# A transformer block on one core: the router's logits taken from scaled rows while the output projection still runs

## Chip, cores and metric

One core of a Trainium2 chip runs the whole block in one launch. The metric is the device time of that launch in microseconds (us), lower is better. The engines are TensorE (PE, its weight loads PEld), VectorE (DVE), ScalarE (ACT), GpSimd (POOL) and SyncE (SP), which issues nearly all transfers.

## What is computed

256 tokens of width 2048 go through an adaptive layer norm, a token mixer (window attention and a gated delta rule, merged and put through `w_out`), a residual norm, a second adaptive norm, a mixture of 32 experts with two experts for each token, and a last residual norm.

```python
u = layer_norm(x) * (1.0 + sc1) + sh1
mix = token_mixer(u, ...)                        # ends in merged @ w_out
x = layer_norm(DEEPNORM_ALPHA * x + g1 * mix, ln1_g, ln1_b)      # "first residual norm"
u = layer_norm(x) * (1.0 + sc2) + sh2
ffn = hier_moe(u, ...)       # router logits -> group, two experts -> gate_up, silu, down
x = layer_norm(DEEPNORM_ALPHA * x + g2 * ffn, ln2_g, ln2_b)
```

Everything is float32. The expert weights are 384 tiles of 1 MB; every expert is computed with 64 slots.

## The kernel before

Tokens lie in two tiles of 128 partitions (`NT` = 2). The stages around the change:

- **Output projection** (`out_todo`, L929). Four column blocks c of 512; each is made of 16 half tiles of `w_out`, and each half tile is split by ACT (`wh`, L288) and DVE (`wl`, L289) into a high and a low part, so that PE computes three products for each (`mx`, L293 to L295). `run` (L375) walks the 32 jobs; while it runs, five expert tiles are fetched ahead (`load_ahead`) and the last part of the modulation (`ada`, L236) is summed on DVE.
- **evac(c)** (L1007). Out of PSUM: `mt` = product times g1 (L1011), `x` = ALPHA x + mt (L1012), sums for the norm (`bn_stats`, L1013). At c = 1 `router_prep` (L983) turns the modulation and the router weights into `br`, `ncs`, `wsel`.
- **The chain to the router** (L1038 to L1092). Once all four blocks are there: mean and 1/std of each token (`both`), then for each c and token tile `x` = (x - mean) ln1_g (L1059) and `x` = x rs + ln1_b (L1060), transposes (L1063), copies into `uq` (L1064), squares on ACT (L1066), logit products (L1053), and a second mean and 1/std from the products' extra column and from the squares. The logits `L` come out at L1090.
- **Routing** (L1128 to L1161): tied maxima, masks, ranks; then `slots` (L1208) makes the 0/1 matrices `G`.
- **xh** (L1101): the twice normalised rows, on ACT, and `g2b` (L1005).
- **Experts.** 16 pairs. `gather` (L1229) makes `XT` = xh-transposed by G in four steps of 8 products (L1236); `gate_up` (L1247) uses 16 weight tiles, `down` (L1288) eight. For pair 0 the gather's steps 1 to 3 stand before k = 2, 6 and 10 of `gate_up` (`GS`). For the other pairs the gather runs between `gate_up` and `down` of the pair before.

Expert tiles go through 17 buffers in a fixed rotation: four of `wp` (L74), six of `wm` (L1325), seven of `wm1` (L1338), issued in program order of use. Five of `wm1` hold the tiles fetched ahead; two hold `l1`, the rows ln1_g and ln1_b (loaded at L1019), until L1060 has read them.

The framework (Tile) orders the instructions of each engine at build time: of those whose inputs are ready it takes the one that stands first in the program. The kernel writes orders by hand only through `run`.

Of the kernel before, what the change touches and what calls it, by code (L numbers as in the profile page):

```python
# [16 lines left out]
P = 128  # L17
# [46 lines left out]
def tile_block(ctx: ExitStack, tc: tile.TileContext, A: dict, out: bass.AP, dbg=None, upto=99):  # L64
# [17 lines left out]
    rows = cp.tile([16, 512], F32, name="rows")  # L82
# [8 lines left out]
    nc.scalar.dma_start(rows, A["lnr"])  # L91
# [70 lines left out]
    def pg(nm):  # L162
        return ps_g.tile([P, 512], F32, tag="g", name=nm)
# [749 lines left out]

    mo = ctx.enter_context(tc.tile_pool(name="mo", bufs=1, reuse_waits="tile"))
# [5 lines left out]
    rw = rwx.enter_context(tc.tile_pool(name="rw", bufs=1, side=R, reuse_waits="tile"))  # L920
    ahead = []

    def load_ahead():
        n = len(ahead)
        w = wm1.tile([P, 2048], F32, tag="w1", name="w1")
        nc.sync.dma_start(w, A["w_gu"][n])
        ahead.append(w)
# [32 lines left out]
    sb = mo.tile([P, NT, 4, 6], F32, name="sb")  # L960
    g2b = mo.tile([P, D], F32, name="g2b")
    L = mo.tile([P, NT, 36], F32, name="L")
    br = rw.tile([P, 36], F32, name="br")
    ncs = rw.tile([P, 36], F32, name="ncs")
    wsel = rw.tile([P, 37], F32, name="wsel")
    rin = rw.tile([P, RW], F32, name="rin")
    nc.sync.dma_start(rin, A["router"])

    def RI(n):
# [4 lines left out]
    l1 = []  # L974
# [7 lines left out]
    def router_prep():  # L982
        mod2 = rw.tile([P, KT, 2], F32, name="mod2")  # L983
# [5 lines left out]
        V.tensor_tensor(wr, wr, sc2c.unsqueeze(2).to_broadcast([P, KT, 64]), op=MUL)  # L989
        G.memset(wr[:, :, 36:37], 1.0)  # L990
        V.tensor_add(wsel, ident[:, 0:37], ident[:, 64:101])
        rc = rw.tile([36, 2], F32, name="rcol")
        V.tensor_copy(rc, pb[:36, 0:2])
        pb = ps_w.tile([P, 512], F32, tag="ws", name="pbr2")
        for j in range(2):
            T.matmul(pb[:, 64 * j:64 * j + 36], rc[:, j:j + 1].to_broadcast([36, P]), ident[:36, :36],
                     start=True, stop=True)
        V.tensor_tensor(br, pb[:, :36], RI("br"), op=ADD)
        V.tensor_scalar(ncs, pb[:, 64:100], -1.0, None, op0=MUL)

    def g2_rows(cs):
        for c in cs:
            p = ps_w.tile([P, 512], F32, tag="ws", name=f"g2{c}")
            spread(p, mrs[5], 32 * c)
            SC.copy(g2b[:, c * 512:(c + 1) * 512], p)  # L1005

    def evac(c, ps):  # L1007
        cs = slice(c * 512, (c + 1) * 512)
        for t in range(NT):
            mt = rw.tile([P, 512], F32, tag="mt", name=f"mt{c}{t}", bufs=2)  # L1010
            V.tensor_tensor(mt, ps[t], gc[c], op=MUL)  # L1011
            V.scalar_tensor_tensor(x[t][:, cs], x[t][:, cs], ALPHA, mt, op0=MUL, op1=ADD)  # L1012
            V.bn_stats(sb[:, t, c, :], x[t][:, cs])  # L1013
        if c < 3:
            g1_row(c + 1)
        if c == 0:
            for q in (0, 4):
                w = wm1.tile([P, D], F32, tag="w1", name=f"l1{q}")
                nc.sync.dma_start(w, A["lnr"][q:q + 4, :].rearrange("a b -> (a b)").partition_broadcast(P))  # L1019
                l1.append(w)  # L1020
        if c == 1:
            while 4 not in mrs:
                next(ada)
            router_prep()

    g1_row(0)
    out_todo()
    run(None, 0, ADA[4])
# [9 lines left out]

    for _ in ada:
        pass  # L1040
    mv, rs = both(sb, "b")
    s2 = mo.tile([P, NT, 4], F32, name="s2")
    nb1 = mo.tile([P, 1], F32, name="nb1")
    V.tensor_reduce(nb1, l1[1], axis=AX.X, op=ADD)
    V.tensor_scalar(nb1, nb1, -1.0 / D, None, op0=MUL)
    pl = ps_w.tile([P, 512], F32, tag="ws", name="pl")
    uqs = []

    def logits(c):
        for k in range(4):  # L1050
            K = 4 * c + k
            j = 64 * (k % 2)
            T.matmul(pl[j:j + 64, :S], wr[:, K, :], uqs[c][:, k, :], start=(K < 2), stop=(K >= KT - 2))  # L1053

    for c in range(4):
        cs = slice(c * 512, (c + 1) * 512)
        uq = rw.tile([P, 4, S], F32, tag="uq", name=f"uq{c}", bufs=2)
        for t in range(NT):
            V.scalar_tensor_tensor(x[t][:, cs], x[t][:, cs], mv[:, t, 0:1], l1[0][:, cs], op0=SUB, op1=MUL)  # L1059
            V.scalar_tensor_tensor(x[t][:, cs], x[t][:, cs], rs[:, t], l1[1][:, cs], op0=MUL, op1=ADD)  # L1060
            p = pg(f"ut{t}{c}")
            for k in range(4):
                T.transpose(p[:, k * P:(k + 1) * P], x[t][:, (4 * c + k) * P:(4 * c + k + 1) * P], ident)  # L1063
            SC.copy(uq[:, :, t * P:(t + 1) * P], p.rearrange("p (k s) -> p k s", k=4))  # L1064
            scr = rw.tile([P, 512], F32, tag="mt", name=f"sq{c}{t}", bufs=2)
            SC.activation(scr, x[t][:, cs], AF.Square, bias=nb1, accum_out=s2[:, t, c:c + 1])  # L1066
        uqs.append(uq)
        if c:
            logits(c - 1)
    logits(3)  # L1070
# [3 lines left out]
    for t in range(NT):  # L1074
        T.matmul(pl[:, 64 * t:64 * t + 37], lt[:, t * P:(t + 1) * P], wsel, start=True, stop=True)
    for t in range(NT):
        dump(f"x1{t}", x[t])

    mv, dv, sv, rs = [mo.tile([P, NT, 1], F32, name=f"{n}c") for n in ("mv", "dv", "sv", "rs")]
    V.tensor_reduce(sv[:, :, 0], s2, axis=AX.X, op=ADD)  # L1080
    py = pl[:, 0:128].rearrange("p (t c) -> p t c", t=NT)[:, :, 36:37]
    V.tensor_scalar(dv, py, 1.0 / D, nb1, op0=MUL, op1=ADD)
    V.tensor_scalar(mv, py, 1.0 / D, None, op0=MUL)
    V.tensor_tensor(dv, dv, dv, op=MUL)
    V.scalar_tensor_tensor(sv, sv, 1.0 / D, dv, op0=MUL, op1=SUB)
    SC.activation(rs, sv, AF.Sqrt, bias=epsl)
    V.reciprocal(rs, rs)
    for t in range(NT):
        V.scalar_tensor_tensor(L[:, t, :], ncs, mv[:, t, 0:1], pl[:, 64 * t:64 * t + 36], op0=MUL, op1=ADD)
        V.scalar_tensor_tensor(L[:, t, :], L[:, t, :], rs[:, t], br, op0=MUL, op1=ADD)  # L1090
    nmr = mo.tile([P, NT, 1], F32, name="nmr")
    V.scalar_tensor_tensor(nmr, mv[:, :, 0:1], -1.0, rs, op0=MUL, op1=MUL)  # L1092
    rs2 = rs
# [6 lines left out]
    for t in range(NT):  # L1100
        SC.activation(xh[t], x[t], AF.Identity, bias=nmr[:, t], scale=rs2[:, t])  # L1101
        g2_rows((2 * t, 2 * t + 1))
# [53 lines left out]
    for t in range(NT):  # L1156
        p = pm(f"rk{t}")
        T.matmul(p[:, :NE], C("lt"), msk[:, t, :], start=True, stop=(t == 0))
        if t:
            T.matmul(p[:, :NE], ones, msk[:, 0, :], start=False, stop=True)  # L1160
        V.scalar_tensor_tensor(pos[:, t, :], msk[:, t, :], -4096.0, p[:, :NE], op0=MUL, op1=ADD)  # L1161

# [66 lines left out]
    def gather(pr, Gs):  # L1229
        XT = mo.tile([P, KT, P], F32, tag="XT", name=f"XT{pr}")  # L1230

        def step(kq):
            p = pm(f"xg{pr}_{kq}")
            for k in range(4):
                for t in range(NT):
                    T.matmul(p[:, k * P:(k + 1) * P], xh[t][:, (4 * kq + k) * P:(4 * kq + k + 1) * P],  # L1236
                             Gs[t].bitcast(F32), start=(t == 0), stop=(t == NT - 1))
            for k in range(4):
                K = 4 * kq + k
                if kq % 2:  # L1240
# [280 lines left out]
def pack(inp):  # L1521
# [44 lines left out]
    wr = np.concatenate([wr, np.zeros((D, 28), np.float32)], 1)  # L1566
# [33 lines left out]
```

## Time and profile before

| | |
|---|---|
| median of 3 runs | 1809.97 us (1809.28 to 1811.17) |
| profiled execution | 1810.3 us, span 1808.4 us, clock 0.985 |
| PE, PEld busy | 1726.9 us (95%), 1106.4 us (61%) |
| DVE, ACT busy | 895.6 us (50%), 516.9 us (29%) |
| HBM read | 624.65 MB, 347 GB/s over the span |

Busy time is that of one profiled execution. A busy PE is not PE at its peak, since the ends of its pipelined products are modelled; the starts tell its pace.

### The profile page before, as it was taken

The page shows a single profiled execution, that of the slowest core. Times are in us where ns is not written, and L with a number is a line of the kernel's source. Part 1 is how long each engine was busy: PE and PEld are TensorE (multiplying, and loading weights), DVE is VectorE, ACT ScalarE, POOL GpSimd, SP SyncE. Part 2 cuts the span into 40 slices and gives each one's busy share as a digit, 9 for nine tenths or more (in the row PEclk, how much of TensorE's full clock was granted, in tenths as well). Part 3 has the DMA queues.
Part 4 walks back from the last instruction along what each step waited for, and adds up shares of the span by engine and source line. Part 5 has one row for each costly group of instructions (what it writes and reads, how often), then busy time and mean ns, then how long its engine had stood idle before and what let it go on. Part 6 is the DMA issues. An engine that isn't in the chain of part 4 may idle for free. (4 is left out here: it accounts for less than half of the span.)

```text
span 1808.4 us, 27501 instructions
## 1 busy us (share of the span) xinstructions
PE 1726.9 (95%) x11526; PEld 1106.4 (61%) x11526; DVE 895.6 (50%) x1454; ACT 516.9 (29%) x955; POOL 43.4 (2%) x50
## 2 busy tenths in 40 slices
PE   7999998999999999997999999999999999999995
PEld 4779887898999999885434444344434444343331
DVE  3356897798788788666223322233213321233026
ACT  3334798336333544435100110011100110011101
POOL 0000001103000000000000000000000000000000
PEclk8999998999999999999999999999999999999998
DMA  9995565465788688978999999999999999999995
GB/s 397 420 362 209 199 254 192 163 258 205 282 288 319 233 303 317 364 263 323 368 421 420 421 420 420 421 421 420 420 421 420 421 420 421 420 420 421 394 422 223
DMA packets 87287, 628.58 MB, mean 348 GB/s; under 512 B 9828, under 2 KB 9828, under 8 KB 11252
## 3 DMA queue, kind: packets, MB, share of 16 engines
q1 hardware_dynamic: 86832, 626.43, 86.4%
q8 instruction: 92, 1.51, 0.3%
q10 hardware_dynamic: 328, 0.36, 0.1%
q14 instruction: 35, 0.29, 0.0%
HBM read 624.65 MB, written 2.10 MB: 347 GB/s over the span
## 5 line engine op out<-in xcount | busy, mean ns | idle before, releaser
L1257 PE MATMUL pg<-w,XT 128*64 128x512 f32 x1024 | 278.5, 599 | 3.4 <-DMA w<-in_w_gu 2.5
L1257 PE MATMUL pu<-w,XT 128*64 128x512 f32 x1024 | 275.5, 594 | 0.0
L293 PE MATMUL ws<-uh,wh 128*128 128x256 f32 x896 | 259.4, 290 | 2.3 <-ACT wh L288 2.3
L288 ACT CAST wh<-w 128x1024 fp32r<-128x1024 f32 x176 | 184.6, 1050 | 257.3 <-PE ws L294 122.2
L295 PE MATMUL ws<-uh,wl 128*128 128x256 f32 x896 | 254.0, 284 | 4.3 <-DVE wl L289 4.3
L294 PE MATMUL ws<-ul,wh 128*128 128x256 f32 x896 | 253.7, 283 | 0.0
L289 DVE TENSOR_TENSOR wl<-w,wh 128x1024 fp32r<-128x1024 f32 x176 | 218.7, 1243 | 52.4 <-PE mx L294 22.8
L1295 PE MATMUL pd<-w,hT 128*64 128x512 f32 x1016 | 234.1, 599 | 0.8 <-DVE hT L1272 0.8
L1264 DVE TENSOR_TENSOR hs<-hs,pu 128x512 f32<-128x512 f32 x16 | 11.0, 687 | 430.3 <-PE pu L1257 430.3
L293 PEld LDWEIGHTS ws<-uh,wh 128*128 128x128 f32 x896 | 169.3, 189 | 12.4 <-issue 7.8
L295 PEld LDWEIGHTS ws<-uh,wl 128*128 128x128 f32 x896 | 169.1, 189 | 6.6 <-DVE wl L289 5.7
L236 DVE SCALAR_TENSOR_TENSOR acc<-w,csil,acc 128x1024 f32<-128x1024 f32 x128 | 165.3, 1307 | 12.6 <-DMA w<-in_w_ada 12.3
L294 PEld LDWEIGHTS ws<-ul,wh 128*128 128x128 f32 x896 | 169.3, 189 | 1.4 <-issue 1.2
L1257 PEld LDWEIGHTS pu<-w,XT 128*64 128x64 f32 x1024 | 77.8, 137 | 146.6 <-issue 146.6
L1257 PEld LDWEIGHTS pg<-w,XT 128*64 128x64 f32 x1024 | 72.5, 137 | 133.6 <-issue 114.0
L1236 PEld LDWEIGHTS xg<-G,xh 128*128 128x128 f32 x1024 | 120.0, 193 | 41.3 <-issue 25.8
L1295 PEld LDWEIGHTS pd<-w,hT 128*64 128x64 f32 x1016 | 66.4, 136 | 124.1 <-issue 109.2
L1236 PE MATMUL xg<-G,xh 128*128 128x128 f32 x1024 | 131.7, 283 | 6.9 <-DVE x L1312 3.5
L1263 ACT ACTIVATE hs<-pg 128x512 f32<-128x512 f32 x16 | 9.6, 598 | 438.5 <-PE pg L1257 438.5
L410 ACT CAST dh<-pd 128x512 fp32r<-128x512 f32 x64 | 37.6, 587 | 281.3 <-DVE pd L1298 160.8
L1298 DVE SCALAR_TENSOR_TENSOR pd<-pd,wsl,g2b 128x512 f32<-128x512 f32 x64 | 48.5, 758 | 104.0 <-PE pd L1295 104.0
L1312 DVE TENSOR_TENSOR x<-x,cb 128x512 f32<-128x512 f32 x120 | 76.9, 682 | 22.7 <-PE cb L1308 22.7
(391 smaller groups left out, 2363.8 us busy)
## 6 DMA issues: line engine op xcount, KB each, us to landing
w<-in_w_gu SPq DMA_DIRECT2D x256, 1024.0 KB, 19.8
w<-in_w_dn SPq DMA_DIRECT2D x127, 1024.0 KB, 19.8
w<-in_w_ada SPq DMA_DIRECT2D x64, 1024.0 KB, 5.1
w<-in_w_in SPq DMA_DIRECT2D x56, 1024.0 KB, 5.1
wx<-in_w_a SPq DMA_DIRECT2D x18, 1024.0 KB, 11.1
w<-in_w_pab SPq DMA_DIRECT2D x16, 1024.0 KB, 6.0
w<-in_w_out SPq DMA_DIRECT2D x16, 1024.0 KB, 4.9
w<-in_w_a SPq DMA_DIRECT2D x14, 1024.0 KB, 10.7
```

Source lines behind the costliest of these rows:

```text
L236: V.scalar_tensor_tensor(acc[:, hc], w[:, hc], csil[:, k:k + 1], acc[:, hc], op0=MUL, op1=ADD)
L288: SC.copy(h, w)
L289: V.tensor_tensor(lo, w, h.bitcast(F32), op=SUB)
L293: T.matmul(p, a[0], b[0], start=first, stop=False)
L294: T.matmul(p, a[0], b[1], start=False, stop=False)
L295: T.matmul(p, a[1], b[0], start=False, stop=last)
L410: SC.copy(h, src)
L1236: T.matmul(p[:, k * P:(k + 1) * P], xh[t][:, (4 * kq + k) * P:(4 * kq + k + 1) * P], Gs[t].bitcast(F32), start=(t == 0), stop=(t == NT - 1))
L1257: T.matmul(dst[64 * e:64 * e + 64, :], XT[:, k, 64 * e:64 * e + 64], we[:, e * 1024 + hv * 512:e * 1024 + hv * 512 + 512], start=(k == 0), ...
L1295: T.matmul(pd[64 * e:64 * e + 64, :], hT[:, f, 64 * e:64 * e + 64], we[:, (2 * (f % 2) + e) * 512:(2 * (f % 2) + e + 1) * 512], start=(f = ...
L1298: V.scalar_tensor_tensor(pd, pd, ws, g2b[:, cs], op0=MUL, op1=MUL)
L1312: V.tensor_tensor(x[t][:, cs], x[t][:, cs], p, op=ADD)
```

## The change

The rows that go to the router are no longer normalised first. `evac(c)` now writes `x` = (x - mu0) ln1_g, with mu0 the mean of the first column block alone, and takes the squares of that; transposes and logit products of block c are put into the jobs of block c + 1 (`beside`). What the true mean, 1/std and ln1_b add to the logits is put in afterwards with constants that `router_prep` computes (`cons`, from extra columns of the router weights), in 15 small DVE instructions ahead of the second root. `router_prep` moves from c = 1 to c = 0. The first gather takes the unfinished `x` with G times a token factor, and adds what is missing with a product of 17 rows (`rows`, `r17`); behind each of its four steps `x` is finished on DVE and `xh` written on ACT. `l1` is therefore read until pair 0's third step. The PSUM pools are opened anew ahead of the projection (four `pg` buffers instead of five, one for `pl`).

```diff
+    early = [wm1.tile([P, 2048], F32, tag="w1", name="w1") for _ in AHEAD]
...
+    for q in (0, 4):
+        w = wm1.tile([P, D], F32, tag="w1", name=f"l1{q}")
+        nc.sync.dma_start(w, A["lnr"][q:q + 4, :].rearrange("a b -> (a b)").partition_broadcast(P))
+        l1.append(w)
...
     def router_prep():
+        V.tensor_reduce(nb1, l1[1], axis=AX.X, op=ADD)
...
+        for k in range(KT):
+            T.matmul(pb[:39, 0:3], wr[:, k, :39], wr[:, k, 36:39], start=(k == 0), stop=(k == KT - 1))
...
+        for j in range(4):
+            T.matmul(pb[:, 64 * j:64 * j + 39], rc[:, j:j + 1].to_broadcast([39, P]), ident[:39, :39],
                      start=True, stop=True)
...
     def evac(c, ps):
...
             V.bn_stats(sb[:, t, c, :], x[t][:, cs])
+            if c == 0:
+                V.bn_aggr(mu0[:, t, :], sb[:, t, 0:1])
+            V.scalar_tensor_tensor(x[t][:, cs], x[t][:, cs], mu0[:, t, 0:1], l1[0][:, cs], op0=SUB, op1=MUL)
+            SC.activation(mt, x[t][:, cs], AF.Square, accum_out=s2[:, t, c:c + 1])
+            todo.append(lambda t=t: turn_part(c, t))
...
+        if c == 2:
+            SC.activation(epst, epsl, AF.Sqrt)
+        todo.append(lambda: logits(c))
...
-    run(None, 0, ADA[4])
+    run(beside(), 1.0, ADA[4], drain=False)
...
-            V.scalar_tensor_tensor(x[t][:, cs], x[t][:, cs], mv[:, t, 0:1], l1[0][:, cs], op0=SUB, op1=MUL)
-            V.scalar_tensor_tensor(x[t][:, cs], x[t][:, cs], rs[:, t], l1[1][:, cs], op0=MUL, op1=ADD)
...
+    g2_rows(range(4))
...
+    stt(one(q2), col(37), nd, one(sv))
+    stt(one(pa), lambda t: cons[:, 1], nd, lambda t: pt[t])
+    stt(one(pa), one(pa), rs, lambda t: cons[:, 2])
+    stt(one(q2), one(q2), rs, col(38))
+    V.tensor_scalar(nm, pa[:, :, 36:37], -1.0 / D, None, op0=MUL)
+    stt(one(q2), pcol(37), nd, one(q2))
+    V.tensor_tensor(dv, nm, nm, op=MUL)
+    stt(one(q2), one(q2), rs, pcol(38))
+    V.scalar_tensor_tensor(sv, q2, 1.0 / D, dv, op0=MUL, op1=SUB)
+    SC.activation(rs2, sv, AF.Sqrt, bias=epsl)
...
-        SC.activation(xh[t], x[t], AF.Identity, bias=nmr[:, t], scale=rs2[:, t])
...
+    def first_gather(Gs):
...
+            V.tensor_scalar(Gp[:, t], Gs[t].bitcast(F32), ag[:, t], None, op0=MUL)
...
+                T.matmul(p[:17, kq * P:(kq + 1) * P], vk[:, t, 17 * kq:17 * kq + 17], Gs[t].bitcast(F32),
+                         start=(t == 0), stop=(t == NT - 1))
...
+        SC.copy(r17, p[:17, :])
...
+            for t in range(NT):
+                T.matmul(p, x[t][:, (4 * kq + k) * P:(4 * kq + k + 1) * P], Gp[:, t], start=(t == 0), stop=False)
+            T.matmul(p, rows[:, k * P:(k + 1) * P], r17[:, kq * P:(kq + 1) * P], start=False, stop=True)
...
+                V.scalar_tensor_tensor(x[t][:, cs], l1[0][:, cs], nd[:, t], x[t][:, cs], op0=MUL, op1=ADD)
+                V.scalar_tensor_tensor(x[t][:, cs], x[t][:, cs], rsb[:, t], l1[1][:, cs], op0=MUL, op1=ADD)
+                SC.activation(xh[t][:, cs], x[t][:, cs], AF.Identity, bias=nmr[:, t], scale=rs2[:, t])
```

## Rows read from the trace of the kernel before

**Rows 1.** Busy time by stretch: us, busy of each engine, PEclk, DMA share, GB/s

```profile
800.00:810.00 10.00, 10.00 (x44) 7.92 (x43) 7.62 (x10) 4.05 (x5) 0.00 (x0) 1.00 0.72 254
...
850.00:855.00 5.00, 4.50 (x22) 3.05 (x23) 1.55 (x10) 2.50 (x8) 0.00 (x0) 0.68 0.01 2
...
898.00:900.00 2.00, 2.00 (x14) 1.21 (x15) 1.52 (x5) 0.21 (x1) 0.00 (x0) 1.00 0.06 25
902.00:904.00 2.00, 2.00 (x12) 0.63 (x10) 0.90 (x2) 0.59 (x1) 0.00 (x0) 1.00 0.83 344
...
1200.00:1400.00 200.00, 195.41 (x962) 82.14 (x960) 52.01 (x101) 18.49 (x40) 0.00 (x0) 1.00 1.01 420
```

**Rows 2.** ACT in order of time: start, duration, once a pair after gate_up

```profile
1003.84 0.60 ACT L1263 ACTIVATE hs<-pg 128x512 f32<-128x512 f32 x1 [30.12 <-PE pg L1257]
...
1524.78 0.60 ACT L1263 ACTIVATE hs<-pg 128x512 f32<-128x512 f32 x1 [29.89 <-PE pg L1257]
1584.70 0.60 ACT L1263 ACTIVATE hs<-pg 128x512 f32<-128x512 f32 x1 [31.93 <-PE pg L1257]
```

**Rows 3.** Waits of PEld from 1500 to 1600: us, times, longest

```profile
PEld pg L1257 <- DMA w<-in_w_gu: 4.4, 4, 1.4
```

**Rows 4.** PE in the projection, in order of time

```profile
777.52 0.39 PE L295 MATMUL mx<-wh,ml 128*128 128x512 f32 x1
777.84 0.63 PE L996 MATMUL pbr<-cst,rcol 36*128 36x36 f32 x4
778.40 0.50 PE L293 MATMUL mx<-wh,mh 128*128 128x512 f32 x1
...
757.82 1.28 PE L988 MATMUL pbr<-mod,rin 128*36 128x2 f32 x32
759.03 0.50 PE L294 MATMUL mx<-wl,mh 128*128 128x512 f32 x1
```

**Rows 5.** The projection's first product, one near the end, the last, of 384

```profile
730.61 0.79 PE L293 MATMUL mx<-wh,mh 128*128 128x512 f32 x1
...
820.05 0.39 PE L295 MATMUL mx<-wh,ml 128*128 128x512 f32 x1
...
822.77 0.39 PE L295 MATMUL mx<-wh,ml 128*128 128x512 f32 x1
```

**Rows 6.** The chain from the projection to the first gate_up, in order of time

```profile
822.52 1.37 DVE L1011 TENSOR_TENSOR mt<-mx,gc 128x512 f32<-128x512 f32 x2 [1.28 <-PE mx L295]
...
835.82 1.42 DVE L1060 SCALAR_TENSOR_TENSOR x<-x,rsb,l 128x512 f32<-128x512 f32 x2
...
837.15 1.09 PE L1063 MATMUL ut<-cst,x 128*128 128x128 f32 x8
...
838.17 1.94 PE L1053 MATMUL pl<-uq,rin 128*64 128x256 f32 x14
...
841.25 0.22 DVE L1082 TENSOR_SCALAR dvc<-plt,nb 128x2 f32<-128x2 f32 x1 [1.43 <-PE plt L1075]
...
842.46 0.42 DVE L1090 SCALAR_TENSOR_TENSOR L<-L,rsc,br 128x36 f32<-128x36 f32 x2
...
842.87 0.22 DVE L1128 TENSOR_REDUCE mg<-L 128x1 f32<-128x4 f32 x2
...
847.81 0.49 DVE L1208 TENSOR_TENSOR G<-pos,cst 128x128 fp32r<-128x128 f32 x2
848.82 3.44 PEld L1236 LDWEIGHTS xg<-G,xh 128*128 128x128 f32 x20 [0.31 <-ACT xh L1101]
...
853.05 1.15 PE L1257 MATMUL pg<-w,XT 128*64 128x512 f32 x4 [0.50 <-ACT XT L1244]
```

**Rows 7.** Pair 0 on PE: step 3 of the gather

```profile
874.04 2.05 PE L1236 MATMUL xg<-G,xh 128*128 128x128 f32 x16
```

**Rows 8.** SP's issues: start, time until the last of the group, tile

```profile
717.73 14.57 SPq L74 DMA_DIRECT2D w<-in_w_out  x5
732.35 0.90 SPq L917 DMA_DIRECT2D x<-in_x  x2
```

More of the change, by code (lines that the diff above doesn't have):

```diff
@@ L81, in tile_block @@
     cst = cp.tile([P, CW], F32, name="cst")
-    rows = cp.tile([16, 512], F32, name="rows")
+    rows = cp.tile([17, 512], F32, name="rows")
+    nc.gpsimd.memset(rows, 1.0)
     pre = ExitStack()
@@ L924, in load_ahead @@
         n = len(ahead)
-        w = wm1.tile([P, 2048], F32, tag="w1", name="w1")
-        nc.sync.dma_start(w, A["w_gu"][n])
-        ahead.append(w)
+        nc.sync.dma_start(early[n], A["w_gu"][n])
+        ahead.append(early[n])
     def out_todo():
@@ L1001, in g2_rows, with turn_part @@
+        V.tensor_tensor(br, cons[:, 3, :36], RI("br"), op=ADD)
     def g2_rows(cs):
         for c in cs:
-            p = ps_w.tile([P, 512], F32, tag="ws", name=f"g2{c}")
+            p = pg(f"g2{c}")
             spread(p, mrs[5], 32 * c)
             SC.copy(g2b[:, c * 512:(c + 1) * 512], p)
+    uqs, todo = [], []
+    pl = ps_l.tile([P, 512], F32, name="pl")
+    def turn_part(c, t):
+        if t == 0:
+            uqs.append(rw.tile([P, 4, S], F32, tag="uq", name=f"uq{c}", bufs=2))
+        p = ps_w.tile([P, 512], F32, tag="ws", name=f"ut{t}{c}")
+        for k in range(4):
+            T.transpose(p[:, k * P:(k + 1) * P], x[t][:, (4 * c + k) * P:(4 * c + k + 1) * P], ident)
+        SC.copy(uqs[c][:, :, t * P:(t + 1) * P], p.rearrange("p (k s) -> p k s", k=4))
@@ L1007, in evac, with logits @@
+    def logits(c):
+        for k in range(4):
+            K = 4 * c + k
+            j = 64 * (k % 2)
+            T.matmul(pl[j:j + 64, :S], wr[:, K, :], uqs[c][:, k, :], start=(K < 2), stop=(K >= KT - 2))
     def evac(c, ps):
@@ L1024, in evac, with beside @@
             router_prep()
+        if c == 2:
+            SC.activation(epst, epsl, AF.Sqrt)
+        todo.append(lambda: logits(c))
+    epst = mo.tile([P, 1], F32, name="epst")
+    def beside():
+        while True:
+            if todo:
+                todo.pop(0)()
+            yield
     g1_row(0)
     out_todo()
-    run(None, 0, ADA[4])
+    run(beside(), 1.0, ADA[4], drain=False)
     def both(sv, nm):
@@ L1037, in both @@
         return mv, rs
+    for f in todo:
+        f()
+    mv, rs = both(sb, "b")
     for _ in ada:
         pass
[L1041 to L1058, printed above, removed]
-            V.scalar_tensor_tensor(x[t][:, cs], x[t][:, cs], mv[:, t, 0:1], l1[0][:, cs], op0=SUB, op1=MUL)
-            V.scalar_tensor_tensor(x[t][:, cs], x[t][:, cs], rs[:, t], l1[1][:, cs], op0=MUL, op1=ADD)
[L1061 to L1070, printed above, removed]
     lt = rw.tile([P, S], F32, name="lt")
@@ L1084, in tile_block @@
[L1084 to L1092, printed above, removed]
@@ L1093, in tile_block @@
-    rs2 = rs
+        T.matmul(pl[:, 64 * t:64 * t + 39], lt[:, t * P:(t + 1) * P], wsel, start=True, stop=True)
+    g2_rows(range(4))
+    nd, sv, q2, nm, dv, rs2, nmr, ag = [mo.tile([P, NT, 1], F32, name=f"{n}c")
+                                       for n in ("nd", "sv", "q2", "nm", "dv", "rs2", "nmr", "ag")]
+    pa = rw.tile([P, NT, 39], F32, name="pa")
+    pt = [pl[:, 64 * t:64 * t + 39] for t in range(NT)]
+    V.tensor_reduce(sv[:, :, 0], s2, axis=AX.X, op=ADD)
+    V.tensor_tensor(nd, mu0[:, :, 0:1], mv[:, :, 0:1], op=SUB)
@@ L1099, in tile_block @@
     xh = [mo.tile([P, D], F32, name=f"xh{t}") for t in range(NT)]
-    for t in range(NT):
-        SC.activation(xh[t], x[t], AF.Identity, bias=nmr[:, t], scale=rs2[:, t])
-        g2_rows((2 * t, 2 * t + 1))
+    vk = mo.tile([P, FF], F32, tag="hs", name="vk")[:, :NT * 68].rearrange("p (t c) -> p t c", t=NT)
+    G.memset(vk, 0.0)
     pps.close()
@@ L1440, in tile_block @@
             Gs = slots(pr, pair(pr)[0])
-            XT, step = gather(pr, Gs)
+            XT, step = first_gather(Gs)
             step(0)
```

99 lines of the change are left out of this document (67 added, 32 removed).

## The prediction, made before the changed kernel ran

> **What bounds the kernel now.** I read the busy time by stretch first. From 904 us to 1782 us the transfers never rest: 420 GB/s, DMA share 1.01, with PE busy for 195 of 200 us beside them [rows 1]. So both are near their limit, and the next view has to tell which one sets the pace. The reader is to look at the instruction that ends `gate_up`, once a pair: nine periods from 1003.84 to 1524.78 take 57.88 us each, the next takes 59.92 [rows 2]. A pair needs 24 tiles of 1024 KB; at 420 GB/s that is 24 x 2.50 = 59.9 us. So PE runs faster than the supply for eleven pairs, eats the stock of up to 17 loaded tiles, and is held by the transfers from pair 12 on, where PEld waits 4.4 us for `w_gu` [rows 3]. The end therefore hangs on the time at which the transfers became continuous. That is 902.3: in the 2 us before 900 they stood (share 0.06), and in 902 to 904 they had 0.83 of the time [rows 1]. They stood because all 17 buffers were full while PE did pair 1's gather, and went on when PE had used pair 0's first `down` tile. **So the place that decides is the time at which PE reaches pair 0's `down`;** what shifts that shifts the whole rest. The other rest of the transfers, 850 to 855 (0.01), is also that of full buffers, and loading earlier is not to be had there.
>
> Three stretches of PE lead there. In the output projection PE is full (10.00 of 10) [rows 1]: its products start 0.2267 us apart (12 of them from 820.05 to 822.77), 384 of them are 87.1 us, and the stretch from 730.61 to 823.0 is 92.4 us [rows 5]; the router's and `gc`'s pieces fill nearly all the rest. In the chain, from 823.0 to 853.05, PE mostly waits for DVE [rows 6]. In pair 0 PE is full again.
>
> **The change, part by part.** I call 823.0 E.
>
> *Moved into the projection* (PE, full, so on the path). 24 of the 32 transposes: eight take 1.09 us with the last one's own 0.34 in it, so 0.108 each [rows 6], 2.6 us. 24 of the 32 logit records: fourteen in 1.94 with a last one of 0.39, so 0.12 each [rows 6], 2.9 us. The second set of router products, 32 records of few columns like those at 757.82, which cost 1.21 [rows 4]: 1.2 us. Four more records of `pbr3`: 0.5 us. Breaking into the stream costs too: between 777.52 and 778.40 four records took 0.88 - 0.23 = 0.65 [rows 4], about 0.13 more than their pace, and there are nine such groups, 1.2 us. Sum **8.4 us**. Bounds: 7.2 without the breaks; above, DVE gets 1.4 us more work in each `evac` and `router_prep` comes in c = 0, so that PE may wait for `wl` up to 1 us in each of three blocks, 11.4. I take 8.4, since PE's own rows carry it.
>
> The Trainium skill (TensorE: Matmul & The Clock Gate, Part 4: PE-mode transpose) gives about 275 ns for a transpose in a kernel. By that, an estimate, 24 of them would be 6.6 us and the stretch 4 us longer than by the row. The row decides: the durations overlap, and the pace is 0.108.
>
> *The chain on DVE.* Before: from the first `mt` (822.52) to the last L1060 (837.24), 14.7 us, and 4.0 more until the transposes, copies, logits and selection let L1082 start at 841.25 [rows 6]. After: two each of `mt`, `x`, `bn_stats` and the scaled step, at 0.64 us, 5.1 us, so E + 4.6; the tail of 4.0 stays as it is for the last block: E + 8.6 instead of E + 18.25. *Gain 9.65.* Then the corrections: L1082 to the first maximum took 1.62 us [rows 6]. Now nine dependent steps stand before the root, mostly of two small instructions; two of 36 columns take 0.42, a single narrow one 0.13 to 0.22 [rows 6], so about 2.2 us, and root, reciprocal and the last two 1.15: 3.35. *Loss 1.7.* Six more small ones for `vk` and `ag` ahead of `G`, partly in PE's turns there, *loss 0.3*, and the root may queue behind a `g2b` copy on ACT, *loss 0.2*. `G` stands at E + 17.8 instead of E + 25.3 (848.30): **gain 7.5**. Bounds 6.5 to 8.5.
>
> *From G to the first gate_up.* Before 4.75 us (848.30 to 853.05), with 20 loads in 3.44, 0.17 each at a clock that fell to 0.68 in that stretch [rows 1, 6]. After: 16 records for the 17 rows, a copy on ACT that the first row product waits for (0.2 beyond the products before it), 24 records instead of 16, and `XT`'s first part, 0.5. The wait for `xh` on ACT goes. 40 records at 0.12 are 4.8, at 0.17 6.8 us; PE is idle longer before it than now, so I take the second: 7.5 in all, **loss 2.75**, bounds 0.9 and 4.5. First `gate_up`: E + 25.3 against E + 30.05, 4.75 earlier.
>
> *Pair 0.* Each of steps 1 to 3 gets eight more records. Sixteen take 2.05 us with a last one of 0.28, 0.118 each [rows 7], so 0.95 for eight: **2.85 us** for three steps, on a full PE. The DVE and ACT work behind each step (four DVE instructions of 0.7, two on ACT) lies beside `gate_up`, where DVE and ACT have over 80% free; if that cover were gone, `XT` of the next step would come up to 2.8 us late.
>
> *Transfers.* `l1` now keeps two of the 17 buffers until step 3 is done. 15 tiles instead of 17 are there when PE starts. That costs nothing as long as SP passes the two loads that need those buffers and goes on with `wp` and `wm`, which come free from k = 5 on: at 2.50 us a tile they keep the transfers busy, and by pair 0's `down` the buffers are full again, about 2.5 us ahead. That SP's order does so is seen at the projection: the two loads of x, first in the program, wait for room, and five `w_out` loads stand before them [rows 8]. The memset ahead of `rows`, the new PSUM pools and the early Sqrt table go with nothing on the path; their bound is 0.3 us.
>
> Sum at pair 0's `down`: +8.4 - 4.75 + 2.85 = **+6.5 us**, and as much at the end. 1810.3 (span 1808.4 and 1.9 around it) + 6.5 = 1816.8; the profiled run is 0.3 above the median, so 1816.5. With the bounds of each (7.2 to 11.4; gain 3 to 7.6; 2.5 to 3), its own range is 1812.5 to 1821.
>
> **The rivals.** A measurement of this kernel can tell 0.2%, 3.6 us, from no change.
>
> *A: SP stands at `l1`'s buffers.* If the loads keep their program order, the sixth load after the fetched stock (tile 20) waits for step 3 and its DVE work: PE's step 3 began 21 us after the first `gate_up` [rows 6, 7] and would end at 26, DVE 3.5 later, landing begins 1.5 after that, at 31. First `gate_up` is then at 856.7, so tile 20 starts at 887.7; continuous from 902.3 with tile 33 means 869.8 for tile 20 now. 17.9 us later, and nothing gives it back: 1828. For it: the rotation is fixed and SP is one queue. Against: [rows 8].
>
> *B: the moved pieces cost little, and the kernel is not slower.* Place: the projection, at each `evac`. If the pieces fill time in which PE would wait for DVE's `wl` anyway, as 2.2 us of `gc` and router products did around 757.82 [rows 4], half of the 8.4 is covered: 4.2 - 4.75 + 2.85 = +2.3, 1812. It decides as soon as the projection grows by less than 5.5 us; free altogether it gives 1808, with a full clock at the first gather 1806. Against: outside that place the products stand 0.2267 apart without a hole. A rule speaks for it: the Trainium skill (Trainium Kernel Development and Optimization, Performance Expectations) calls matmul busy time a bad metric and asks for the share of the weight loads; that is 79% in this stretch, so a fifth would be free for the 8.4 us, and the result would be B's. The spacing of the starts in the rows speaks against it.
>
> *C: the pieces are not where the program puts them,* but run after E, where PE has 4.6 us of waiting for DVE. Then the projection grows by the router's 1.9 alone and the chain by what does not fit into the wait, 1 to 2 us: 1.9 + 1.5 - 4.75 + 2.85 = +1.5, 1811.5. Against: they become ready a block earlier, and what is ready and first in the program goes first.
>
> **How the numbers follow.** Forecast 0.70 (1816.5), A 0.12 (1828), B 0.13 (1812, with 0.05 of it at 1806 or below), C 0.05 (1811.5). The range 1810 to 1825 holds nearly all of the forecast, C and most of B, and leaves out A and B's lowest part. Slower by over 0.2%: the forecast without its lowest tenth, and A, 0.75; faster by over 0.2%: B's lowest part, 0.06; within: 0.19.
>
> **What would show it.** Right: the projection, first to last product, 8 us longer, with transposes and `pl` records between its products; first maximum 12 us after its end, `G` at 18, `gate_up` at 25; pair periods unchanged; the transfers' second rest still there, about 6 us later. Wrong: a projection under 98 us (B, C), or SP standing at a `wm1` load while `wp` is free and a rest of over 8 us during pair 0's `gate_up` (A). If DVE is what the first gather waits for, the corrections were priced too low.

## The result, and the profile after

The changed kernel takes 1828.76 us (median of four runs, 1823.19 to 1834.54) against 1809.62 for the kernel before beside it: ratio 1.0105, interval 1.0073 to 1.0138. It is slower, as forecast, but by 19 us where 6.5 were forecast, outside the range of 1810 to 1825. The profiled execution is the slowest of the four: 1834.5 us, span 1832.7, mean granted clock 0.979. One execution of one variant below was disturbed (4794 us) and is left out.

All stations below are counted from the projection's first product, since its start differs from profile to profile: 728.8 and 731.1 in two of the changed kernel as it is, 728.8 to 736.4 over its variants, 730.6 to 733.0 in the three of the kernel before and its variants. What moves it is open.

| us after the projection's first product | before | after | difference | forecast |
|---|---|---|---|---|
| last product of the projection | 92.2 | 105.5 | +13.3 | +8.4 |
| first maximum of the router | 112.3 | 118.3 | +6.1 | |
| `G` | 117.2 | 124.0 | +6.8 | +0.9 |
| first `gate_up` | 122.4 | 137.3 | +14.9 | +3.65 |
| pair 0's `down` | 168.1 | 192.1 | +24.0 | +6.5 |
| end of the span | 1077.8 | 1101.7 | +23.9 | +6.5 |

The loss is complete at pair 0's `down`, and from there to the end nothing is added. ACT once a pair, after `gate_up` (start, duration), against [rows 2]:

```profile
1028.24 0.60 ACT L1345 ACTIVATE hs<-pg 128x512 f32<-128x512 f32 x1 [30.13 <-PE pg L1339]
...
1491.03 0.60 ACT L1345 ACTIVATE hs<-pg 128x512 f32<-128x512 f32 x1 [29.89 <-PE pg L1339]
1549.60 0.60 ACT L1345 ACTIVATE hs<-pg 128x512 f32<-128x512 f32 x1 [30.60 <-PE pg L1339]
```

1028.24 against 1003.84 is 24.4 later, 1549.60 against 1524.78 is 24.8. The eight periods up to 1491.03 are 57.85 us each, as before; then the supply of weights sets the pace, as before (the next but one takes 60.84, against 59.92).

**The projection.** The four blocks (from `mt` to `mt`) took 23.83, 22.59 and 22.66 us before; now 32.17, 24.87 and 24.87. So block 1 alone lost 8.3 us, the other two 2.3 and 2.2. Block 1 in order of time on DVE (first the kernel before, then the changed one), on PE, and by stretch (us, busy of PE, PEld, DVE, ACT, POOL, PEclk, DMA share, GB/s):

```profile
751.25 2.28 DVE L1044 TENSOR_REDUCE nb<-l 128x1 f32<-128x2048 f32 x1
...
757.03 2.35 DVE L289 TENSOR_TENSOR wl<-w,wh 128x1024 fp32r<-128x1024 f32 x2
```

```profile
752.17 2.28 DVE L1000 TENSOR_REDUCE nb<-l 128x1 f32<-128x2048 f32 x1
...
760.37 1.21 DVE L290 TENSOR_TENSOR wl<-w,wh 128x1024 fp32r<-128x1024 f32 x1
```

```profile
760.61 1.33 PE L1017 MATMUL pbr<-rin 128*39 128x3 f32 x32 [1.26 <-ACT mt L1061]
761.87 0.79 PE L295 MATMUL mx<-wl,mh 128*128 128x512 f32 x1
...
766.21 0.63 PE L296 MATMUL mx<-wh,ml 128*128 128x512 f32 x1
766.64 0.63 PE L294 MATMUL mx<-wh,mh 128*128 128x512 f32 x1
```

```profile
755.00:760.00 5.00, 4.34 (x41) 3.40 (x39) 5.00 (x13) 2.38 (x4) 0.00 (x0) 1.00 1.01 421
760.00:765.00 5.00, 4.39 (x44) 3.89 (x45) 3.30 (x7) 1.21 (x4) 0.00 (x0) 0.69 0.59 202
765.00:770.00 5.00, 5.00 (x19) 4.10 (x18) 0.64 (x2) 1.54 (x3) 0.00 (x0) 0.63 0.15 61
```

From 752.17 to 760.37 DVE writes no `wl`: the sum over `l1`, `evac(0)` with its new scaled step, and the router's instructions stand in one row of 8.2 us. Before, the sum over `l1` stood at the same place, and the row was 5.8 us long; the 2.4 us are the scaled step with its mean and the router's DVE work, which came behind two `wl` then (it stood at c = 1 in the program, but ran in this block all the same). PE runs out of work around 760 (1.26 idle), and the granted clock falls to 0.69 and 0.63 in the next two stretches; the products at 766 start 0.43 apart instead of 0.2267 [rows 5].

**The chain.** DVE and PE from the logits' selection to the first `gate_up`, and the busy time by stretch there:

```profile
846.19 0.34 DVE L1115 SCALAR_TENSOR_TENSOR q2c<-plt,ndc,svc 128x1 f32<-128x1 f32 x2 [1.89 <-PE plt L1103]
...
849.38 0.21 DVE L1168 TENSOR_REDUCE mg<-L 128x1 f32<-128x4 f32 x2
```

```profile
853.45 1.06 PE L1198 MATMUL rk<-msk,cst 128*128 128x32 f32 x4 [7.29 <-DVE msk L1178]
...
855.51 3.57 PE L1297 MATMUL rk<-G,vk 128*17 128x128 f32 x16 [0.57 <-DVE G L1255]
859.01 1.22 PE L1304 MATMUL xg<-Gp,x 128*128 128x128 f32 x4
860.16 0.79 PE L1305 MATMUL xg<-r,rows 17*128 17x128 f32 x2
860.89 1.22 PE L1304 MATMUL xg<-Gp,x 128*128 128x128 f32 x4
...
868.38 1.98 PE L1339 MATMUL pg<-w,XT 128*64 128x512 f32 x4
```

```profile
850.00:855.00 5.00, 1.49 (x6) 1.35 (x6) 4.03 (x40) 1.58 (x3) 0.00 (x0) 0.50 1.00 415
...
860.00:865.00 5.00, 5.00 (x17) 3.71 (x16) 0.00 (x0) 0.00 (x0) 0.00 (x0) 0.50 0.00 0
865.00:870.00 5.00, 5.00 (x16) 3.01 (x17) 2.74 (x4) 2.90 (x6) 0.00 (x0) 0.50 0.02 3
```

The reader is to see two things. PE stood for 7.29 us ahead of the ranks, and the granted clock falls to 0.50, that is 1.2 GHz, during this wait (0.72 in 845 to 850) and stays there until 871.1, after the first `gate_up` products: every record of the first gather runs at 1.2 GHz. And PE takes the gather as four records of 128 rows and two of 17 rows in turn, 1.88 us for each such six.

**Pair 0's step 1,** at full clock, beside which [rows 7] had sixteen records in 2.05 us:

```profile
873.28 0.71 PE L1304 MATMUL xg<-Gp,x 128*128 128x128 f32 x4
873.93 0.48 PE L1305 MATMUL xg<-r,rows 17*128 17x128 f32 x2
874.34 0.71 PE L1304 MATMUL xg<-Gp,x 128*128 128x128 f32 x4
```

1.055 us for each six, four times a step: 4.2 us where 1.98 + 0.95 was forecast. The starts within a six tell where it goes: records of one shape follow each other every 0.112 us, six of them 0.67; the other 0.385 falls on the two changes of shape, 0.19 each.

### The profile page after: what moved, and what is told of

It reads as the page before. It is cut to its first block, busy times and chain, and to the rows that moved or that the text cites. A ratio compares the mean times of both kernels' runs of the same rounds, so it can differ in the third digit from the quotient of the medians.

```text
span 1832.7 us, 27708 instructions
## 1 busy us (share of the span) xinstructions
PE 1747.9 (95%) x11610; PEld 1121.1 (61%) x11610; DVE 902.6 (49%) x1485; ACT 517.9 (28%) x963; POOL 46.1 (3%) x53
## 5 line engine op out<-in xcount | busy, mean ns | idle before, releaser
L1377 PEld LDWEIGHTS pd<-w,hT 128*64 128x64 f32 x1016 | 66.4, 136 | 124.0 <-issue 109.4
L1283 PEld LDWEIGHTS xg<-G,xh 128*128 128x128 f32 x960 | 112.8, 194 | 37.8 <-issue 22.7
L1283 PE MATMUL xg<-G,xh 128*128 128x128 f32 x960 | 123.3, 283 | 6.1 <-DVE x L1394 3.5
```

Of the source, the lines that this page charges most:

```text
L1377: T.matmul(pd[64 * e:64 * e + 64, :], hT[:, f, 64 * e:64 * e + 64], we[:, (2 * (f % 2) + e) * 512:(2 * (f % 2) + e + 1) * 512], start=(f = ...
```

## The experiments

One table holds the stations of every kernel that ran (us after the first product of the projection; the last column is from `down` to the end of the span).

| kernel | last product | first maximum | G | first gate_up | down | down to end | median us | ratio to before |
|---|---|---|---|---|---|---|---|---|
| before | 92.2 | 112.3 | 117.2 | 122.4 | 168.1 | 909.6 | | |
| after | 105.5 | 118.3 | 124.0 | 137.3 | 192.1 | 909.6 | 1828.8 | 1.0105 |
| l1 held in the kernel before | 92.2 | 112.6 | 117.6 | 122.8 | 168.4 | 910.0 | 1813.2 | 1.0011 |
| rows last | 105.4 | 118.3 | 124.0 | 132.5 | 181.4 | 909.5 | 1824.8 | 1.0080 |
| pieces late | 97.5 | 113.9 | 119.6 | 129.4 | 182.7 | 909.9 | 1826.6 | 1.0096 |
| router early | 103.1 | 115.9 | 121.6 | 131.4 | 184.7 | 910.3 | 1829.4 | 1.0102 |
| PE kept busy | 104.1 | 117.2 | 122.3 | 130.0 | 183.2 | 909.6 | 1826.1 | 1.0096 |
| no 17-row products | 105.7 | 118.5 | 124.2 | 130.0 | 175.7 | 912.5 | 1824.1 | 1.0068 |
| three mended | 103.1 | 116.2 | 121.3 | 129.0 | 179.2 | 910.2 | 1821.6 | 1.0061 |
| all late | 95.8 | 111.2 | 116.3 | 122.5 | 172.9 | 909.6 | 1815.7 | 1.0025 |
| changed again | 104.1 | 116.9 | 122.6 | 135.9 | 190.9 | 909.6 | 1829.6 | 1.0112 |
| x finished early | 95.9 | 115.1 | 120.1 | 124.8 | 171.7 | 908.5 | 1812.4 | 1.0020 |
| before, PE kept busy | 92.2 | 112.5 | 121.1 | 128.4 | 175.3 | 908.4 | 1815.9 | 1.0031 |
| x behind G | 95.0 | 111.1 | 116.3 | 120.3 | 166.4 | 908.9 | 1810.4 | 0.9992 |

The last column stays between 908.4 and 910.3 while `down` moves by 26 us, but for one kernel (912.5, explained there). That the time of pair 0's `down` sets the end, the base of the forecast, is shown.

**Rival A: `l1`'s buffers held, in the kernel before.** The fetched tiles get their buffers early, and two small additions behind step 3 read `l1`, so that two buffers are kept until then and nothing else changes.

```diff
+                    if pr == 0 and K == 15:
+                        for j in range(2):
+                            V.tensor_tensor(junk, l1[j][:, 0:1], p[:, 511:512], op=ADD)
```

> The kernel before, with one thing of the change: the five buffers for the tiles fetched ahead are taken first and l1's two last, and both rows of l1 are read once more, a single column each, by DVE behind step 3 of pair 0's gather, so that their buffers come free only then. Rival A (SP stands at these buffers, or two tiles fewer in stock cost the end): 12 to 18 us over the kernel before, 1822 to 1828. Theory 1 (SP passes on to other buffers, and the stock is full again by pair 0's down): within 1.5 us of the kernel before.

1813.24 us, ratio 1.0011 (0.9996 to 1.0026); the median is 3.1 us over the kernel before beside it (1810.18), and whether anything of that is a cost is not resolved. A would have given 1822 to 1828. A falls, although the changed kernel's median is A's number to the microsecond: the number came about by other terms. SP's issues in this kernel, then in the changed one (start, time until the last of the group):

```profile
867.81 4.18 SPq L74 DMA_DIRECT2D w<-in_w_dn  x2
...
880.25 0.80 SPq L1342 DMA_DIRECT2D w<-in_w_dn  x2
```

```profile
883.58 6.41 SPq L74 DMA_DIRECT2D w<-in_w_dn  x2
891.38 2.04 SPq L74 DMA_DIRECT2D w<-in_w_gu  x2
901.77 1.12 SPq L1420 DMA_DIRECT2D w<-in_w_dn  x2
902.98 5.12 SPq L1407 DMA_DIRECT2D w<-in_w_gu  x6
```

SP does pass the two loads (the pair at 880.25 and at 901.77) with `wp`'s, as [rows 8] suggested; `wm`'s six come behind them. So half of A's mechanism is there, and it costs a short rest of the transfers (in the changed kernel a share of 0.41 in 900 to 905), not 17.9 us.

**The row products at the end of each step.** All sixteen products of 128 rows first, then the eight of 17; the marks that start and stop the sum in PSUM move with them.

```diff
+            for k in range(4):
+                row_products(p[:, k * P:(k + 1) * P], kq, k)
```

> One thing is changed in the changed kernel: in each step of the first gather the four 17-row products stand behind the eight 128-row products of the step, not one behind every two. Theory 1 (PE pays for each switch between a 128-row and a 17-row product, about 0.17 us at the full clock and 0.3 at the slow one): the steps in pair 0 fall from 4.2 us to about 3.2, the first one from 7.5 to about 5.7, so 4 to 5 us less than the changed kernel, 1824. Rival A (the two buffers that l1 holds set the end): no change from 1829. Rival W (only the number of records counts): no change.

1824.82 us (1824.2 to 1827.07), 4 us less, and `down` at +181.4 instead of +192.1. One step on PE:

```profile
879.81 2.05 PE L1304 MATMUL xg<-Gp,x 128*128 128x128 f32 x16
881.79 1.15 PE L1307 MATMUL xg<-r,rows 17*128 17x128 f32 x8
```

Sixteen records as in [rows 7], and eight in 1.1: the forecast's price for the records, 0.95, holds. What it left out is the taking in turn: 4.22 - 3.07 = 1.15 us a step, for six changes of shape fewer, so again 0.19 a change. The Trainium skill (TensorEngine Tiling (Array Packing), Key Properties) says that a change of the tiling mode, not of the tile alone, drains TensorE; it gives no price. These rows fit it and give a price, 0.19 us a change; that a product of 17 rows puts TensorE into another mode is shown by no run here. The prediction did not weigh this page. That it is the shape and not the breaking in is seen in the changed kernel's projection, at full clock:

```profile
793.86 0.39 PE L294 MATMUL mx<-wh,mh 128*128 128x512 f32 x1
794.09 0.60 PE L1040 MATMUL ut<-cst,x 128*128 128x128 f32 x4
...
794.75 0.39 PE L296 MATMUL mx<-wh,ml 128*128 128x512 f32 x1
...
796.14 0.39 PE L296 MATMUL mx<-wh,ml 128*128 128x512 f32 x1
796.46 1.08 PE L1047 MATMUL pl<-uq,rin 128*64 128x256 f32 x8
...
797.81 0.40 PE L295 MATMUL mx<-wl,mh 128*128 128x512 f32 x1
```

Four transposes of the same `128*128` take 0.89 - 0.45 = 0.44 us, their pace of 0.108 and nothing for the change; eight logit products of `128*64` take 1.67 - 0.45 = 1.22, at their pace of 0.108 (two start every 0.216) 0.86, so 0.35 for the two changes.

**PE kept busy in the chain.** Seven idle products of 512 columns behind the selection of the logits, nothing else.

```diff
+    pw = ps_a.tile([P, 512], F32, tag="ada", name="pw")
+    for _ in range(7):
+        T.matmul(pw, lt[:, 0:P], g2b[:, 0:512], start=True, stop=True)
```

> One thing is added to the changed kernel: seven products of 512 columns whose result nobody reads, behind the selection of the logits, so that PE works for 6 us of the 7.4 us in which it idles before the ranks. Theory 1 (PE's idle time drops it to the slow clock, at which the first gather and the first expert tile then run): the granted clock from the first rank product to the first gate_up is near 1.0 instead of 0.5; from G to the first gate_up 8 us instead of 12.8; the kernel 4 to 7 us faster than the changed one, 1822 to 1825, and its runs closer together. Rival W (the records themselves): no change or slower. Rival A: no change.

The first `gate_up`, at a granted clock of 1.00 from 840 to 870:

```profile
861.34 1.08 PE L1342 MATMUL pg<-w,XT 128*64 128x512 f32 x4
```

`G` to the first `gate_up` takes 7.63 us instead of 13.3, and `down` comes at +183.2: the mechanism is as expected. The time is not: three runs gave 1824.2, 1826.1 and 1832.3, ratio 1.0096 (1.0067 to 1.0126), not 1822 to 1825. The gain seen in the profile is not resolved in the times.

**The changed kernel once more,** because two other kernels that leave the gather as it is had it in 9.8 us.

> The changed kernel once more, nothing edited. Theory now: the first profile (span 1832.7) caught the longest of the spread that the granted clock makes in block 1 of the projection and in the first gather. The runs with one part undone that keep the first gather as it is (the router's products in block 1, and the pieces behind the projection) showed G to first gate_up in 9.8 us instead of 13.3, and pair 0's down at first product + 182.7 to 184.7 instead of + 192.1. So another profile should show 9.5 to 10.5 us there, down at + 183 to + 187, and span minus the time of down again 909.5 to 910.5; time 1823 to 1829. Rival: the 13.3 us and the + 192 belong to the kernel as it is and come again; then the parts undone had gained 8 to 10 us each, though they do not touch the gather.

1829.58 us (1825.82 to 1835.71), and the rival held: 13.3 us again, `down` at +190.9. So the first profile was no accident. Here it is again at a clock of 0.50, where with the pieces late the clock is back within the second group:

```profile
855.30 1.22 PE L1304 MATMUL xg<-Gp,x 128*128 128x128 f32 x4
...
857.18 1.22 PE L1304 MATMUL xg<-Gp,x 128*128 128x128 f32 x4
```

```profile
853.39 1.22 PE L1304 MATMUL xg<-Gp,x 128*128 128x128 f32 x4
854.54 0.56 PE L1305 MATMUL xg<-r,rows 17*128 17x128 f32 x2
855.03 0.71 PE L1304 MATMUL xg<-Gp,x 128*128 128x128 f32 x4
```

PE's work before and after the pause is of the same kind in both. Why the full clock returns there after about 5 us and here after 16 is not settled by these runs. The times of the eight runs of the changed kernel follow their mean granted clock, from 1823.19 us at 0.986 to 1835.71 at 0.978.

**The pieces behind the projection** (transposes and logit products no longer put between its jobs):

```diff
-    run(beside(), 1.0, ADA[4], drain=False)
+    run(None, 0, ADA[4])
```

> One thing is changed in the changed kernel: the transposes and logit products of all four blocks stand in the program behind the whole projection, so that PE takes them only where a projection product is not ready, or after the last one. Theory 1: blocks 2 and 3 fall back from 24.9 us to about 22.6 each, most of the records then run after the last product, beside DVE's 4.6 us of evacuation; first gate_up 2 to 4 us earlier, 1825 to 1827. If they fill holes in the stretch of evac(0) alone, the gain is 5. Rival A: no change.

1826.62 us. The projection is 8.0 us shorter (6.6 against the second profile of the changed kernel, in which the clock of block 1 fell for half as long) and the chain to the first maximum 3.6 us longer (16.4 instead of 12.85 in both). So the same pieces cost 6.6 to 8.0 us in the projection and 3.6 behind it, where PE waits for DVE anyway; by these profiles, moving them in was a loss of 3.0 to 4.4 us by itself.

**The router's products ahead of the projection's loop in program order** (so that they are not tied to `evac(0)`):

```diff
-        if c == 0:
-            while 4 not in mrs:
-                next(ada)
-            router_prep()
+    while 4 not in mrs:
+        next(ada)
+    router_prep()
```

> One thing is changed in the changed kernel: the router's preparation is called before the first job of the projection instead of in evac(0). Theory 1 (in evac(0) DVE's burst of 9 us leaves PE without split weights, and PE then runs at its slow clock): the time between the evacuations of block 0 and block 1 falls from 32.2 us to about 27, and the kernel by 4 to 6 us, to 1823 to 1825. Rival W (PE's added records are the cost, wherever they stand): no change, 1829. Rival A: no change, since the end hangs on the buffers.

1829.37 us, not the 1823 to 1825 expected. In the profile block 1 is 28.3 us instead of 32.2, at a granted clock of 1.00 from 755 to 770 (one line is under the last heading), but the block ahead of it is 1.5 longer; 2.4 us remain, and the time doesn't show them.

**No 17-row products.** They and their factors are left out, so the first gather lacks what they add.

```diff
-            T.matmul(p, rows[:, k * P:(k + 1) * P], r17[:, kq * P:(kq + 1) * P], start=False, stop=True)
```

> The 17 rows are left out of the changed kernel: the products that make them, their copy, and the 16 products of 17 rows, so the first pair's experts get inputs without mean and shift. Theory 1: G to first gate_up falls from 12.8 us by the rank products (3.6), the copy's wait and the 17-row products of step 0 with their switches (about 4): to 6; the three steps fall from 4.2 us to 2.0, 6.7 us less; in sum 12 to 14 us, 1815 to 1817. By the forecast's prices (16 and 8 records at 0.17, 24 at 0.12) it would be 7 us, 1822. Rival A: no change, 1829.

1824.1 us, not 1815 to 1817. `gate_up` to `down` is 45.8 us, as before the change (45.7), so these products, with their changes of shape and the clock, are the whole of the loss in pair 0. But here `down` to the end is 912.5: `down` comes 16.4 us sooner than in the changed kernel, and the transfers' rest while SP waits for `l1` is then no longer covered:

```profile
890.00:895.00 5.00, 5.00 (x26) 1.65 (x24) 3.44 (x8) 1.63 (x2) 0.00 (x0) 1.00 0.41 147
```

So the held buffers cost nothing as long as PE is late, and by this one profile about 3 us once it is not.

**The mends together.** Rows last, router early and idle products, by the three diffs above; then the pieces late as well, by the fourth.

> The changed kernel with the three edits together: 17-row products last in each step, router preparation before the projection, seven idle products ahead of the ranks. Theory 1: the three gains add, since they lie in three places of one path: 4.5 + 5 + 5.5, 1814, 4 us over the kernel before. Rival A: no change, 1829.

> The same three edits, and the transposes and logit products behind the whole projection. Theory 1: another 2 to 4 us, 1810 to 1812, no measurable difference from the kernel before. If the late pieces do not fit beside DVE's evacuation, as 1814.

1821.61 us against 1814 expected, and 1815.69 (1813.15 to 1819.13) against 1810 to 1812. So the step between the two is 5.9 us where 2 to 4 were expected, and their runs lie apart (1820.07 to 1825.26 the first): that the pieces are cheaper behind the projection is shown by the times too. In the second, `G` stands 0.9 us ahead of the kernel before and the first `gate_up` level with it; what is left are the row products, and a granted clock of 0.50 for 3.4 us in pair 1's gather: 50.4 us from `gate_up` to `down` instead of 45.7.

**A version without them.** `x` is finished on DVE before `xh` is written, column block 0 while DVE waits for the logits, blocks 1 to 3 behind `G`; the first gather is the old one.

```diff
+    finish_x(0)
...
-            XT, step = first_gather(Gs)
+            XT, step = gather(pr, Gs)
             step(0)
+            for c in range(1, 4):
+                finish_x(c)
+                write_xh(c)
```

> All of the change's order mended (router products in block 1 again, transposes and logits behind the projection, idle products in the chain), and the 17-row products gone: x is finished on DVE in 16 instructions of 0.69 us, column block 0 while DVE waits for the last logits, blocks 1 to 3 behind G, xh on ACT after each, and the first gather is the old one with 16 records a step. The computation is whole. Theory (the time of pair 0's down sets the end, the rest of the loss was the 17-row products): G at first product + 116.3 as with the products late, 4.5 to 5 us to the first gate_up instead of 6.2, 45.7 us to down instead of 50.4: down at + 166.5 to + 168, against + 168.1 in the kernel before; time 1807 to 1811 by how late the projection starts. Rival: finishing x belongs in front of G and costs the chain what it cost before (2.8 us for block 0 and whatever the list of ready instructions puts there of the others): G at + 119 or later, 1812 to 1815.

1812.42 us (1810.37 to 1821.06), the rival's value. The list of ready instructions took all sixteen steps in front of the first maximum, twelve of them of blocks 1 to 3; seven stand behind the first use of the selected logits at 838.16, the last four here:

```profile
842.91 1.41 DVE L1118 SCALAR_TENSOR_TENSOR x<-l,ndc,x 128x512 f32<-128x512 f32 x2
844.24 1.41 DVE L1119 SCALAR_TENSOR_TENSOR x<-x,rsb,l 128x512 f32<-128x512 f32 x2
845.56 0.21 DVE L1181 TENSOR_REDUCE mg<-L 128x1 f32<-128x4 f32 x2
```

**The same with these steps forced behind `G`** by a data dependence, and the router's products at c = 1 again.

```diff
+            for dst, src in ((nd2, nd), (rs2b, rsb)):
+                V.scalar_tensor_tensor(dst, pos[:, :, 0:1], 0.0, src, op0=MUL, op1=ADD)
```

> As the kernel without 17-row products, with two edits: column blocks 1 to 3 of x are finished behind G by force (their scalars are copied with a product of the ranks times zero, so they cannot be taken earlier), and the router's products stand at c = 1 as in the kernel before. The computation is whole. Read from the last run: first maximum 3.9 us later after the projection than with the products late (19.2 against 15.3), with eight of the finishing steps of 0.7 us in front of it. Theory (these steps are all that was lost there, and the time of pair 0's down sets the end): last product at first + 93.5 to 95.5, first maximum 15.3 to 15.6 behind it, G 5 later, first gate_up 4.7 later, down 46 to 47 later: first product + 165 to 168 against + 168.1 in the kernel before; time 1807 to 1810.5. Rival (DVE is the bound again once the steps stand behind G): XT of steps 1 to 3 or xh comes late by up to 2.8 us, down at + 168 to + 171, 1810.5 to 1813.

`down` at +166.4, inside the expected 165 to 168 and 1.8 ahead of the kernel before; 1810.36 us against 1811.53 beside it, ratio 0.9992 (0.9981 to 1.0003). No difference that can be measured. The gather there, at full clock:

```profile
849.49 2.02 PE L1293 MATMUL xg<-G,xh 128*128 128x128 f32 x16 [0.57 <-DVE G L1265]
...
853.08 1.08 PE L1317 MATMUL pg<-w,XT 128*64 128x512 f32 x4
```

**Idle products in the kernel before,** at the same place in its chain:

```diff
+    for _ in range(7):
+        T.matmul(pw, lt[:, 0:P], x[0][:, 0:512], start=True, stop=True)
```

> The kernel before with seven idle products of 512 columns behind the selection of the logits, and nothing else. Theory (the clock that falls while PE waits prices the first gather in this kernel too): from G to the first gate_up 3.5 to 4 us instead of 5.2, all later ones as much earlier, 1808 to 1809.5. Rival: the idle products stand in front of the small rank products and cost what they gain: G up to 1 us later, 1810 to 1811.

1815.93 us, slower than either expectation. Behind the idle products stand `g2b`'s, and only then the ranks:

```profile
842.72 6.25 PE L1078 MATMUL pw<-x,lt 128*128 128x512 f32 x14
848.81 3.68 PE L168 MATMUL g<-mr,cst 128*128 128x512 f32 x8
852.33 0.53 PE L1161 MATMUL rk<-msk,cst 128*128 128x32 f32 x4
```

`G` is 3.9 us later, and `xh` on ACT, behind the copies of `g2b`, later still. So idle products cost what they displace, where PE has real products queued for the stretch that they fill.

## Why the prediction was wrong

**Right.** The place that decides, the time of pair 0's `down`; the sign; the chain on DVE: a gain of 9.65 - 1.7 = 7.95 was forecast to the first maximum, 7.25 measured, and the corrections took 3.19 us where 3.35 stood. The price of the pieces in an undisturbed block held too: two blocks of 2.3 and 2.2, where eight transposes, eight logit records and their breaks had been priced at 2.2. B and C fall: the projection grew by 13.3, not by less than 5.5, and the pieces were where the program puts them. But C's own arithmetic, that the pieces would be cheaper behind the projection, is what the runs found. That A's 1828 is the measured median is chance, since its mechanism was tested and cost no such time.

**Wrong, three sizes,** which with the 1.0 us by which the gain up to `G` fell short (6.5 instead of 7.5) make up the 17.5 us between +6.5 and +24.0. What the sum left out is the granted clock after a wait, in all three, and the changes of shape on PE in the last two. Its range was also added up too narrow: the bounds named give a gain of 6.5 - 4.5 = 2.0 at the least, not 3, and an upper end 1 us higher; 1828.76 lies beyond that too.

1. *The projection, +13.3 instead of 8.4.* The step that failed is block 1. "PE may wait for `wl` up to 1 us in each of three blocks" stood as a bound, outside the 8.4, and priced the wait and not what follows it: DVE's row of 8.2 us without a `wl` (5.8 before) left PE idle for 1.26 us, and with the granted clock at 0.69 and 0.63 for 10 us, that is (0.31 + 0.37) x 5 = 3.4 us of full-speed work lost. Together that is 4.7 of the 4.9 us. In the second profile the clock fell for half as long, and the projection grew by 11.9.
2. *From `G` to the first `gate_up`, +8.1 instead of 2.75.* By kernels: 4.0 us for the old gather at full clock (x behind G), 6.2 with the 24 records (eight of them of 17 rows, at the end; all late), 7.63 with them in turn (PE kept busy), 13.3 at half clock. So records 2.2, turns 1.4, clock 5.7; of these 9.3, 1.2 stood in the kernel before, whose 5.2 us were in part at the slow clock. The forecast took 0.17 a record from [rows 6], where the clock was 0.68; it said that PE would be idle for longer and did not price a clock of 0.50.
3. *Pair 0, +9.1 instead of 2.85.* The records cost 3.2 (rows last), near the price; the turns 3 x 1.15 = 3.5, which the forecast had at nothing. The rest, 2.4, is mostly the clock, still at 0.50 until 871.1 and again for 3.4 us in pair 1's gather, which stands before this `down`. (In the three kernels with the same turns and the full clock at the first `gate_up` this stretch takes 53.2 us instead of 54.8.)

By the mends' own kernels: of the 24.0 us at `down`, the taking in turn and the clock behind it are 10.7 (rows last), the pieces' place 3.0 to 4.4, the row products left in pair 0 4.7 (all late, with the fall of the clock in pair 1's gather in it; 3.2 in rows last, without one). These don't add up exactly, since the clock reacts to each of them.

The times say the same in three steps. The ratio to the kernel before goes from 1.0105 (1.0112 in the second set of runs) to 1.0061 with the three mends together, to 1.0025 with the pieces late as well, and to 0.9992 with the row products gone, `x` finished behind `G` and the router's products at c = 1. On 1810 us that is 8.0, 6.5 and 6.0 us, together the whole loss; only the intervals of the first two touch (1.0073 to 1.0138, 1.0043 to 1.0079).

The transfers, priced at nothing, came out at the edge. The sign given for them, their second rest about 6 us later, was not met: around `down` at 923.2 their share was 0.93 on average from 924 to 934, where before it was 0.22, 0.01 and 0.41 in the three 2 us from 897 on. So the held buffers had used up nearly all of the stock's lead, and the run without row products, with `down` sooner, pays 3 us for them.

What stays open is the size in the times. The profiles of both runs of the changed kernel lie above its medians, the first by 5.8 us, and gains of 7 and 9 us at `down` by profile (router early, PE kept busy) were not seen in the medians; rows last has 10.7 by profile and 4 by median. At the clock that the kernel before has, 0.985 and 0.986, the changed kernel still took 1825.8 and 1823.2 us, so most of the loss stands at an equal mean clock too. With a granted clock that differs from run to run, a profile tells the mechanism and the median tells the size.

## What to carry to other kernels

Before work is moved from a chain where an engine waits into a stretch where it is full, price both places: here the pieces cost 6.6 to 8 us in the projection and 3.6 behind it. Where two products of 17 rows stand between products of 128, the changes of shape (0.385 us) cost more than the two records (0.22), so put all of one shape together. And price a wait of PE with what it does to the granted clock of the work behind it: by profile, a pause of 7 us here cost the first gather 5.7 us more.

## What the runs showed of the hardware

- Changing between products of 128 and of 17 rows: 0.19 us a change at full clock (six records in turn 1.055 us, where six at the pace of 0.112 would be 0.67), the same in four kernels. Between products of `128*128` and `128*64` it was 0.35 us for two changes, between products and transposes that are both `128*128` nothing that can be seen.
- A clock at 0.50 under full PE load: PE busy for 5.00 of 5 us in two stretches, 860 to 870, and the clock stayed; in the kernels with the pieces late or the router early the same records had it back after about 5 us.
- After a wait of PE for 1.26 us in block 1 the granted clock was 0.69 and 0.63; in the kernel with the router early PE was busy for 4.17 of 5 us there, less than here (4.39), and the clock stayed at 1.00. So too ahead of pair 1's gather: PE was busy for 3.80 of 5 us in the kernel before (885 to 890) and in the changed one (910 to 915), and the clock was 1.00 and 0.70. What decides between them is not settled. The line of the kernel with the router early:

```profile
760.00:765.00 5.00, 4.17 (x38) 2.85 (x36) 3.19 (x10) 1.89 (x3) 0.00 (x0) 1.00 0.53 220
```
